# A roll along rows, DRAM to DRAM: 528 DMAs of one row per engine become sixteen DMAs of 32 rows per engine

## The chip, the cores and the metric

The kernel runs on one core of one Trainium2 chip. The metric is the device time of one execution in microseconds (us). The kernel before takes 826.24 us, the median of 3 runs (825.08 to 826.99).

A core has compute engines (TensorE, VectorE = DVE, ScalarE = ACT, GpSimd = POOL), SyncE (SP), and 16 DMA engines that copy memory. A DMA is started by an instruction on SP, ACT or POOL; its transfer is then cut into packets that the 16 DMA engines carry out. Here SP and ACT each have one hardware queue, and POOL has a software queue. Almost nothing is computed in this kernel: it is a copy of 268 MB from DRAM to DRAM with every row rotated.

## The reference

```python
def setup_inputs():
    return {
        "x": np.random.randn(8192, 8192).astype(np.float32),
        "shift": 100,
    }

def reference(x: np.ndarray, shift: int) -> np.ndarray:
    return np.roll(x, shift, axis=1)
```

Output column `c` of a row is input column `c - 100`, and the first 100 output columns are the last 100 input columns of the same row. A row has 8192 floats, 32 KB.

## The kernel before

With `shift` 100 the kernel sets `s = 100`, `a = 128` (the shift rounded up to a multiple of 128) and `g = a - s = 28`. Output columns 128 to 8191 are the *long pieces*: 8064 floats (32,256 bytes) of each row, copied from input columns 28 to 8091. Output columns 0 to 127 are the *heads*: 100 floats from the end of the input row and 28 from its start.

**Long pieces (lines 27 to 36).** The rows are taken in 256 blocks of 32. Of a block, the 16 even rows go into one DMA issued by SP and the 16 odd rows into one DMA issued by ACT. In the view `(c e j) w -> c j e w`, `c` is the block, `j` even or odd, and `e` one of 16 rows. As `e` is the slowest dimension of the transfer, each of the 16 DMA engines gets one row of it: one piece of 32,256 bytes. In the last 8 blocks each row is cut in two (columns 128 to 4095 and 4096 to 8191), and each half goes in a DMA of its own. So there are 248 DMAs of whole pieces and 16 of halves on each of the two queues, 528 in all. They run straight from `x` to `out` in DRAM and pass through no on-chip memory.

No line of the kernel waits between these DMAs. The framework gives DMAs on the hardware queues eight semaphores in turn, four for each issuing engine. A DMA may only be issued when the earlier one with the same semaphore has landed on all 16 DMA engines. So each queue has at most four of these DMAs in flight, and the fifth waits for the first.

**Heads (lines 50 to 68).** POOL handles them, 512 rows at a time, in 16 steps of four rows per partition. Line 60 loads a tile `t` of 128 x 3 x 128 floats: a run of 128 floats that begins 100 before a row's end holds the end of one row and the start of the next. Lines 61 and 64 load into the tile `h` what these runs don't hold. DVE copies from `t` to `h` (lines 62 and 65). After all 16 steps, line 68 writes the 16 tiles `h` to the first 128 columns of `out`. These DMAs are issued with `single_packet`, and at most eight are in flight.

Both parts write different columns of `out` and read only `x`, so neither waits for the other. They share the 16 DMA engines and the DRAM.

Of the kernel before, what the change touches and what calls it, by code (L numbers as in the profile page):

```python
# [1 line left out]

# [4 lines left out]


@with_exitstack
def kernel(  # L10
    ctx: ExitStack,
    tc: tile.TileContext,
    x: bass.AP,
    shift: int,
    out: bass.AP,
):
    nc = tc.nc
    n_rows, n_cols = x.shape
    s = shift % n_cols
    a = -(-s // 128) * 128  # L20
    g = a - s
    P = nc.NUM_PARTITIONS
    engines = [nc.sync, nc.scalar]
    n_chunks = 16
    rows = n_rows // n_chunks

    xm = x.rearrange("(c e j) w -> c j e w", e=16, j=2)
    om = out.rearrange("(c e j) w -> c j e w", e=16, j=2)
    if a < n_cols:
        blocks = n_rows // 32  # L30
        mid = (a + n_cols) // 256 * 128
        for c in range(blocks):
            parts = ((a, mid), (mid, n_cols)) if c >= blocks - 8 and a < mid else ((a, n_cols),)
            for j in range(2):
                for lo, hi in parts:
                    engines[j].dma_start(out=om[c, j, :, lo:hi], in_=xm[c, j, :, lo - s:hi - s])
    if a == 0:
        return

    if a > 512:  # L40
        for i in range(n_chunks):
            r = slice(i * rows, (i + 1) * rows)
            nc.gpsimd.dma_start(out=out[r, :s], in_=x[r, n_cols - s:])
            if g > 0:
                nc.gpsimd.dma_start(out=out[r, s:a], in_=x[r, :g])
        return

    Q = 4
    n_st = n_rows // (P * Q)
    reads = ctx.enter_context(tc.tile_pool(name="reads", bufs=n_st))  # L50
    heads = ctx.enter_context(tc.tile_pool(name="heads", bufs=n_st))
    xt = x.rearrange("(k p q) c -> k p q c", q=Q, p=P)
    ot = out.rearrange("(k p q) c -> k p q c", q=Q, p=P)
    tiles = []
    for k in range(n_st):
        t = reads.tile([P, Q - 1, a], x.dtype)
        h = heads.tile([P, Q, a], x.dtype)
        lead = bass.AP(tensor=x.tensor, offset=(k * P * Q + 1) * n_cols - s,
                       ap=[[Q * n_cols, P], [n_cols, Q - 1], [1, a]])
        nc.gpsimd.dma_start(out=t[:], in_=lead, single_packet=True)  # L60
        nc.gpsimd.dma_start(out=h[:, Q - 1, :s], in_=xt[k, :, Q - 1, n_cols - s:], single_packet=True)  # L61
        nc.vector.tensor_copy(h[:, :Q - 1, :s], t[:, :, :s])  # L62
        if g > 0:
            nc.gpsimd.dma_start(out=h[:, 0, s:], in_=xt[k, :, 0, :g], single_packet=True)  # L64
            nc.vector.tensor_copy(h[:, 1:, s:], t[:, :, s:])  # L65
        tiles.append(h)
    for k, h in enumerate(tiles):
        nc.gpsimd.dma_start(out=ot[k, :, :, :a], in_=h[:], single_packet=True)  # L68


# [1 line left out]
_INS = ['x', 'shift']  # L72
_OUTS = [((8192, 8192), 'float32')]

_NUMBERS = {'shift': 100}


# [26 lines left out]
```

## Time and profile before

| | |
|---|---|
| median of the runs | 826.24 us |
| the profiled execution, its own time | 825.38 us |
| its span (first to last instruction) | 823.6 us |
| DRAM read, written | 268.44 MB, 268.44 MB |
| packets on the two hardware queues | 8448 each: 4224 of data, 4224 of 4 bytes |
| packets on POOL's queue | 3328: 2304 of data, 1024 of 4 bytes |
| POOL busy | 41.1 us |
| DVE busy | 7.8 us |

The profile's page gives, for 40 slices of the span, how busy the DMA engines were (9 is 90% or more) and what they moved. It then lists the DMA queues: `q1` and `q10` are the two hardware queues (SP's and ACT's), `q0` is POOL's. A packet of 4 bytes is the write that tells a semaphore that one DMA engine has done its part of a DMA. The list of issues gives for each kind of DMA how many there were, their size, and the median time from issue to landing. GB/s counts each byte moved once; a copy from DRAM to DRAM loads the DRAM with twice that. Besides the page, the trace holds a record of every packet (queue, start, duration, size) and of every write to a semaphore; it does not say which DMA engine a packet ran on.

### The profile page before, as it was taken

Reading aid. Unit: us, or ns where it says so; the run is one execution under the profiler, and the core shown is the slowest. Engines: PE = TensorE matmul, PEld = TensorE weight load, DVE = VectorE, ACT = ScalarE, POOL = GpSimd, SP = SyncE. Lnnn points to the kernel's source line nnn. Section 1 sums busy time; section 2 is a strip of 40 time slices with the busy share of each in tenths; the row PEclk is TensorE's granted clock in tenths of the full one; section 3 lists DMA queues with packets and bytes.
Section 4 is the critical chain, followed back from the end, with each engine's and each line's share of the span. In section 5 each row is a group of like instructions: output and inputs, shape, how many; then the busy total and the mean of one; then the engine's idle time right before and its main releaser. Section 6 shows DMA issues by size and latency. Waiting matters only on the chain. (4 is left out here: it accounts for less than half of the span.)

```text
span 823.6 us, 689 instructions
## 1 busy us (share of the span) xinstructions
DVE 7.8 (1%) x32; POOL 41.1 (5%) x68
## 2 busy tenths in 40 slices
DVE  0000000000000000000000000000000000000000
POOL 3111111211100000000000000000000000000000
DMA  9999999999999999999999999999999999999998
GB/s 300 345 338 345 325 338 340 332 344 359 341 341 345 338 337 323 332 332 321 329 331 331 324 329 331 332 326 329 332 326 329 336 323 337 320 335 337 321 312 302
DMA packets 20229, 272.71 MB, mean 331 GB/s; under 512 B 9472, under 2 KB 9728, under 8 KB 11776
## 3 DMA queue, kind: packets, MB, share of 16 engines
q1 hardware_dynamic: 8448, 132.14, 47.8%
q10 hardware_dynamic: 8448, 132.14, 46.7%
q0 software_dynamic: 3328, 8.39, 4.7%
q14 instruction: 5, 0.04, 0.0%
HBM read 268.44 MB, written 268.44 MB: 652 GB/s over the span
## 5 line engine op out<-in xcount | busy, mean ns | idle before, releaser
L68 POOL DMA_DIRECT2D out_dram<-h x16 | 11.4, 712 | 83.1 <-DMA out_dram<-h 49.6
L60 POOL DMA_DIRECT2D t<-in_x_dram x16 | 12.1, 758 | 32.5 <-DMA h<-in_x_dram 31.6
L64 POOL DMA_DIRECT2D h<-in_x_dram x16 | 8.6, 539 | 80.4 <-DMA t<-in_x_dram 80.4
L61 POOL DMA_DIRECT2D h<-in_x_dram x16 | 8.9, 558 | 20.8 <-DMA h<-in_x_dram 20.8
L62 DVE COPY h<-t 128x300 f32<-128x300 f32 x16 | 5.9, 368 | 179.7 <-DMA t<-in_x_dram 179.7
L65 DVE COPY h<-t 128x84 f32<-128x84 f32 x16 | 3.2, 201 | 0.0
L85 POOL MEMSET const-float32-0.0<- 128x1 f32 x1 | 0.1, 99 | 0.2 <-issue 0.2
L85 POOL MEMSET const-bfloat16-1.0<- 128x1 bf16 x1 | 0.1, 101 | 0.0
L85 POOL MEMSET const-uint8-127<- 128x1 uint8 x1 | 0.1, 99 | 0.0
L85 POOL MEMSET const-float32-1.0<- 128x1 f32 x1 | 0.1, 98 | 0.0
## 6 DMA issues: line engine op xcount, KB each, us to landing
out_dram<-in_x_dram ACTq DMA_DIRECT2D x248, 504.0 KB, 12.6
out_dram<-in_x_dram SPq DMA_DIRECT2D x248, 504.0 KB, 12.6
out_dram<-h POOLq DMA_DIRECT2D x16, 256.0 KB, 64.9
t<-in_x_dram POOLq DMA_DIRECT2D x16, 192.0 KB, 31.6
out_dram<-in_x_dram ACTq DMA_DIRECT2D x8, 256.0 KB, 6.0
out_dram<-in_x_dram SPq DMA_DIRECT2D x8, 256.0 KB, 5.9
out_dram<-in_x_dram ACTq DMA_DIRECT2D x8, 248.0 KB, 6.1
out_dram<-in_x_dram SPq DMA_DIRECT2D x8, 248.0 KB, 6.1
```

The lines of the kernel that those rows point to most:

```text
L60: nc.gpsimd.dma_start(out=t[:], in_=lead, single_packet=True)
L61: nc.gpsimd.dma_start(out=h[:, Q - 1, :s], in_=xt[k, :, Q - 1, n_cols - s:], single_packet=True)
L62: nc.vector.tensor_copy(h[:, :Q - 1, :s], t[:, :, :s])
L64: nc.gpsimd.dma_start(out=h[:, 0, s:], in_=xt[k, :, 0, :g], single_packet=True)
L65: nc.vector.tensor_copy(h[:, 1:, s:], t[:, :, s:])
L68: nc.gpsimd.dma_start(out=ot[k, :, :, :a], in_=h[:], single_packet=True)
L85: nc = _bacc.Bacc("TRN2", target_bir_lowering=False, num_devices=1)
```

## The change

The long pieces are issued as sixteen DMAs, eight by SP and eight by ACT. The rows are taken in 8 blocks of 1024. Of each block a DMA takes all even or all odd rows, `16 x 32` of them: each DMA engine gets 32 pieces, one of each of the 32 former blocks, in the same order. The halves in the last 8 former blocks are gone. The rest of the kernel is unchanged; its line numbers are three lower.

```diff
-    xm = x.rearrange("(c e j) w -> c j e w", e=16, j=2)
-    om = out.rearrange("(c e j) w -> c j e w", e=16, j=2)
     if a < n_cols:
-        blocks = n_rows // 32
-        mid = (a + n_cols) // 256 * 128
-        for c in range(blocks):
-            parts = ((a, mid), (mid, n_cols)) if c >= blocks - 8 and a < mid else ((a, n_cols),)
+        deep = 32
+        xm = x.rearrange("(b c e j) w -> b j e c w", c=deep, e=16, j=2)
+        om = out.rearrange("(b c e j) w -> b j e c w", c=deep, e=16, j=2)
+        for b in range(n_rows // (32 * deep)):
             for j in range(2):
-                for lo, hi in parts:
-                    engines[j].dma_start(out=om[c, j, :, lo:hi], in_=xm[c, j, :, lo - s:hi - s])
+                engines[j].dma_start(out=om[b, j, :, :, a:], in_=xm[b, j, :, :, a - s:n_cols - s])
```

The semaphores are dealt out as before: on each queue the first four DMAs are issued at once, and the fifth waits until the first has landed on all 16 engines.

## The prediction

> **What bounds the kernel now.** I read the page's slices first, then the DMA queues, the waits of SP's queue, stretches of the span by time, and last the trace's records of packets and semaphore writes.
>
> ```profile
> DMA  9999999999999999999999999999999999999998
> GB/s 300 345 338 345 325 338 340 332 344 359 341 341 345 338 337 323 332 332 321 329 331 331 324 329 331 332 326 329 332 326 329 336 323 337 320 335 337 321 312 302
> ...
> q1 hardware_dynamic: 8448, 132.14, 47.8%
> q10 hardware_dynamic: 8448, 132.14, 46.7%
> q0 software_dynamic: 3328, 8.39, 4.7%
> ...
> HBM read 268.44 MB, written 268.44 MB: 652 GB/s over the span
> ```
>
> The DMA engines are busy from end to end (47.8 + 46.7 + 4.7 = 99.2%), at a rate that hardly moves. Nothing else in the program is near a limit. But is it the engines or the DRAM? The packet records decide: an unhindered piece of 32,256 bytes takes 1193 ns (the shortest, and 5% of all), 27.0 GB/s on one engine, 432 GB/s on 16; between 320 and 770 us the mean is 1556 ns, the 95th percentile 2080. So a piece is usually held up by something shared. The stretches say by what:
>
> ```profile
> core 0: us, DVE busy (x) POOL busy (x), PEclk, DMA share, GB/s
> ...
> 20.00:190.00 170.00, 7.28 (x30) 28.11 (x45) 1.00 1.00 339
> 190.00:320.00 130.00, 0.00 (x0) 6.40 (x9) 1.00 1.01 341
> 320.00:794.00 474.00, 0.00 (x0) 0.00 (x0) 1.00 1.00 329
> 794.00:819.50 25.50, 0.00 (x0) 0.00 (x0) 1.00 0.92 313
> 819.50:823.60 4.10, 0.00 (x0) 0.00 (x0) 1.00 0.52 178
> ```
>
> The last two columns are the engines' busy share and GB/s. With POOL's traffic (first two rows) more bytes move, but POOL's bytes touch DRAM once and a long piece's twice; counted by DRAM traffic from the packet records, the rates are about 648, 657 and 658 GB/s. One number fits three mixes: the DRAM side caps the kernel near 658 GB/s, 329 GB/s of copying, and 329/27.0 = 12.2 unhindered engines would be enough to reach it.
>
> ```profile
> SPq L36 <- DMA out_dram<-in_x_dram: 678.2, 260, 4.6
> ...
> out_dram<-in_x_dram ACTq DMA_DIRECT2D x248, 504.0 KB, 12.6
> out_dram<-in_x_dram SPq DMA_DIRECT2D x248, 504.0 KB, 12.6
> ```
>
> SP waited 260 times (264 DMAs less the first four) for an earlier DMA to land: the window of four. It couples the engines. For the 300 DMAs that landed between 320 and 790 us the median spread between the first and the last of the 16 engines is 5.5 us: thirteen within 2.5 us, the last two 3 to 5.5 us behind. The leaders run into the window: from 20 to 790 us about 0.5% of the 16 engines' time has no packet open. Under a cap that costs nothing, as the others take the bandwidth. In the last 25 us the halves shrink the spread to 1.6 us.
>
> **The change, part by part.**
>
> *The floor, unchanged.* 264.2 MB of long pieces at 329 GB/s are 803.2 us; POOL's 8.39 MB at 658 GB/s are 12.8 us. Together 816.0. The span has 7.6 more: the start, 5 x (1 - 206/329) = 1.9 (206 GB/s in the first 5 us), the end, 25.5 x (1 - 313/329) + 4.1 x (1 - 178/329) = 1.2 + 1.9 = 3.1, and 2.6 under POOL's traffic.
>
> *Issues and waits removed:* 256 issues on each of SP and ACT, and 252 waits on each. Nothing else is queued on SP or ACT, and the rings were rarely dry, so 0. From below: the 0.5% idle, 4.1 us, if it was real loss.
>
> *Semaphore writes removed.* Each engine carries two 4-byte packets (about 6 ns each by the starts that follow one another) per pair of pieces; 256 pairs x 12 ns = 3.1 us per engine. Under the cap this is again bandwidth that others use: 0 taken, -3.1 at best.
>
> The Trainium skill's "DMA: Bandwidth & Descriptors" (Rules for kernel authors, with its fit of 2.0 us fixed per DMA) says to move a MiB or more per DMA; 512 DMAs fewer would by that fit be 1024 us of fixed cost, an estimate of 128 us with eight in flight. The trace disagrees: that cost lies under other packets, since the engines idle 0.5%.
>
> *POOL's turns.* A 4-byte packet took a turn on its engine like a piece did: the packet records, followed along one engine, read: a piece of q1, a piece of q10, POOL, 4 bytes of q1, 4 bytes of q10, POOL. So POOL had two turns per pair. It used 3328/16 = 208 turns per engine between 5.3 and 321.1 us, 1.52 us each. With one 4-byte packet in 32 it gets one turn per pair, so 208 of the 256 pairs: its heads last until 640 to 690 us rather than 321. That is still inside the bulk, 130 us early; the cover is the long pieces, and if it went, see the last rival. Cost 0.
>
> *The start.* Which order the descriptors of a deep DMA appear in is not shown. q10's first 16 packets start in two groups 0.66 us apart, at 41 ns per packet if that is generation. From below 0; from above, if the 32 of one engine come before the next engine's, the last engine starts 480 x 0.041 = 20 us late, about +14 at both ends together. The page shows 16 pieces starting inside 0.8 us, the nearest row, so I take 0.
>
> *The end: the window opens.* Four DMAs of 32 pieces on two queues are 256 pieces, 400 us of work: no engine waits for another any more, and each simply has 512 pieces and its POOL packets to do. Pieces vary with a standard deviation of 298 ns (packet records, 330 to 770 us), POOL's 144 data packets per engine with 324 ns. If they vary independently, engines end with a deviation of sqrt(512) x 0.298 = 6.7 and sqrt(144) x 0.324 = 3.9, together 7.8 us. The last of 16 is then some 1.8 deviations, 14 us, behind the mean. Once four engines have finished, the others run unhindered, 1193 instead of 1556 ns; over the last 25 us this wins back 25 x 0.23 = 6. Loss at the end: 14 - 6 = 8 us, in place of 3.1. Bounds: the spread of now, 5.5 us in two engines, loses about 3.2; the largest, a lag that belongs to certain engines, is a rival below.
>
> *Sum* on the profiled execution: 825.4 - 3.1 + 8.0 = 830.3 us, +0.6%. That run lies 0.9 us under the median of 826.24, against which it is +0.5%.
>
> **Rivals.**
>
> *Nothing drifts.* Were the equal mean pace due to the DRAM alone, the spread would stay at 5.5 us: 825.4 - 3.1 + 3.2 = 825.5. For it: the chains of packets that can be followed for 200 us and more have mean pieces of 1550 to 1574 ns, under 2% apart. Against: rings that run dry, so a window that does hold the leaders.
>
> *Faster.* If the engines' own occupancy is the limit and not the DRAM, every gap removed counts: 0.5% idle (4.1), semaphore writes (3.1), the halves' stretch and its end (some 2.5 of 3.1): 825.4 - 9.7 = about 816. It decides if pieces keep their mean of 1556 ns when the gaps are gone. For it: a busy share of 1.00 everywhere. Against: 1193 ns possible, and one DRAM rate in three mixes.
>
> *Slow engines run away.* Between the 12th and 24th DMA (27 to 49 us) the spread grew from 2.2 to 7.0 us, then the window stopped it. About 15 turns of POOL fell in it, 0.33 us per turn; if it is the same few engines each time, the 128 turns of POOL's loads give 128 x 0.33 = 42 us. Three engines 42 us late work alone at the end: some 27 pieces too many each at 1193 ns, 32 us, less what the others did not have to do in the shared stretch, about 8: +24. 825.4 - 3.1 + 24 = 846. For it: the last three of 16 stand apart in every stretch. Against: long POOL packets (275 of 2304 over 500 ns) are found in nearly every chain. The skill's same page (Latency and other measured facts) calls engines 7 and 15 usually slower under descriptors from GpSimd, a best guess there. No record here names an engine, so the trace neither confirms nor denies it.
>
> *POOL starves.* If a queue's turn lasted for all 32 pieces of a DMA, POOL would get 8 turns and do its 200 others behind the bulk: 16 steps of loads and writes with 41.1 us of POOL's own time and landings, some 60 us, less the 12.8 us of DRAM traffic moved there: 825 + 47 = 872. Against: each piece has a packet of its own now.
>
> **How the numbers follow.** Forecast 0.45; nothing drifts 0.17; faster 0.18; run-away 0.13; starved 0.07. Three runs spread by 0.2%, so a change below 0.2%, 824.6 to 827.9, counts as none. Faster: 0.18 + 0.02 of the undrifted = 0.20. Same: 0.14 of the undrifted + 0.06 of the forecast's low end = 0.20. Slower: 0.60. The range reaches from the faster case to the run-away one, 816 to 846, and leaves out the starved case and the far sides; the forecast's own is 826 to 838.
>
> **What would show it.** Right: the same 329 GB/s in mid-run, hardly any 4-byte packets, POOL's last packet at 640 to 690 us, the engines' last landings spread over 15 us or more, and GB/s falling in the last slices. Wrong: a rate above 332 or below 326 GB/s in mid-run (the DRAM cap depends on the order that the window kept), a last landing as tight as now, POOL's packets after the bulk, or a slow first 20 us.

## The result: slower by 3.4%, and the profile after

The changed kernel takes 862.34 us (median of 6 runs, 851.69 to 880.34) against 825.49 us for the kernel before in the same rounds (824.67 to 826.99). The ratio is 1.0338, 95% interval 1.0314 to 1.0363; as its times scatter by 3%, this ratio (and each below that has an interval) is made from the runs within 1.5% of the kernel's fastest, here three of six (851.69 to 856.67), and the ratio of the medians of all runs is 1.045. The profiled execution took 877.91 us, with a span of 876.1: what follows shows the effect at its larger size.

The page of the changed kernel, its slices, packets and queues:

```profile
DMA  9999999999999999999999999999999999998310
GB/s 304 341 324 335 331 334 330 331 336 331 329 336 329 332 331 337 328 334 323 330 330 333 340 334 341 337 335 339 331 338 335 329 319 327 324 327 315 137 46 25
DMA packets 11777, 272.64 MB, mean 311 GB/s; under 512 B 1280, under 2 KB 1536, under 8 KB 3584
...
q10 hardware_dynamic: 4224, 132.12, 44.1%
q1 hardware_dynamic: 4224, 132.12, 43.7%
q0 software_dynamic: 3328, 8.39, 5.2%
```

36 slices run at some 330 GB/s, near the rate before. The last three collapse to 137, 46 and 25 GB/s. The 4-byte packets of the hardware queues are all but gone (1280 packets under 512 bytes, most of them POOL's, where there were 9472), the bytes are the same, and POOL's packets take 5.2% of the engines' time where they took 4.7%. The stretches of the changed kernel (busy share and GB/s in the last columns):

```profile
core 0: us, DVE busy (x) POOL busy (x), PEclk, DMA share, GB/s
640.00:780.00 140.00, 0.00 (x0) 0.00 (x0) 1.00 1.00 328
780.00:800.00 20.00, 0.00 (x0) 0.00 (x0) 1.00 0.98 326
800.00:820.00 20.00, 0.00 (x0) 0.00 (x0) 1.00 0.60 239
820.00:840.00 20.00, 0.00 (x0) 0.00 (x0) 1.00 0.20 87
840.00:860.00 20.00, 0.00 (x0) 0.00 (x0) 1.00 0.09 37
860.00:876.00 16.00, 0.00 (x0) 0.00 (x0) 1.00 0.06 24
```

A busy share of 0.06 is one engine of 16. Against 329 GB/s the rows lose 0.2 + 5.5 + 14.7 + 17.8 + 14.8 = 53 us. The span grew by 52.5, and the end of the kernel before had lost 3.1, so the end accounts for 50 of the 52.5: in the last DMA twelve engines are done between 797 and 822 us, three more by 848, and one works alone until 875.

When they fell apart shows in the writes to semaphores, 16 for each DMA, one by each engine. For the changed kernel's profiled execution, in us of the span (six of the sixteen DMAs; the median engine is the middle of the 16 landings):

| DMA (its last landing) | first to last engine | the last four, behind the median engine |
|---|---|---|
| 115 | 16.6 | 2.0, 4.7, 10.3, 10.7 |
| 237 | 43.0 | 10.7, 22.0, 26.1, 34.8 |
| 361 | 73.0 | 26.5, 27.0, 27.5, 57.9 |
| 488 | 103.0 | 23.7, 24.4, 45.5, 81.7 |
| 592 | 104.4 | 26.6, 27.8, 47.9, 84.1 |
| 796 | 102.3 | 26.4, 26.5, 46.8, 82.0 |

In the kernel before the spread was 5.5 us in mid-run. Here it grows evenly to 488 us and then stops. POOL's last load packet starts at 477 us; its writes go on until 730 us and add nothing. In the packet records many load packets are long: 258 of the 768 of 4096 bytes (34%), and 41% of those of 3200 bytes, take over 500 ns, while the quickest take 159 and 125 ns. They are not spread evenly. The trace doesn't name a packet's engine, but a packet starts within nanoseconds of the end of the one before it on its engine, so chains of packets can be followed, with some wrong links. Between 120 and 240 us the three slowest chains, with load packets of 0.9 to 1.3 us on average, do 0.52 to 0.60 pieces per us; nearly all others, with load packets of 0.25 to 0.6 us, do 0.62 to 0.68. After the loads all packets of POOL take about 159 ns and all chains do 0.62 to 0.63.

### The profile page after: what moved, and what is told of

It reads as the page before. It is cut to its first block, busy times and chain, and to the rows that moved or that the text cites. A ratio compares the mean times of both kernels' runs of the same rounds, so it can differ in the third digit from the quotient of the medians.

```text
span 876.1 us, 177 instructions
## 1 busy us (share of the span) xinstructions
DVE 7.8 (1%) x32; POOL 41.1 (5%) x68
## 2 busy tenths in 40 slices
DMA packets 11777, 272.64 MB, mean 311 GB/s; under 512 B 1280, under 2 KB 1536, under 8 KB 3584
## 4 chain that ended last, share of the span: by engine, by line
another core or an unknown queue 61%; DMA 5%; POOL 1%; issue 1%; DVE 1%; POOLq 0%; DVEq 0%; PEldq 0%
DMA t<-in_x_dram 5%; POOL out_dram L65 1%; DVE h L59 1%; DVE h L62 0%; POOL t L57 0%; POOLq L96 0%; POOL h L58 0%; POOL h L61 0%; POOLq L65 0%; DVEq L96 0%; PEldq L96 0%
```

## Experiments

Theory L, formed from this: POOL's loads are slow on a few DMA engines, these engines fall behind for as long as loads run, and the deep DMAs take away the window that held the others back. The runs were made on several chips (the kernel before takes 815 to 827 us on them), so each is given as a ratio to the kernel before on the same chip.

**1 and 2. Both kernels without the heads.** POOL's and DVE's work is left out.

```diff
-    if a == 0:
-        return
+    return
```

> The changed kernel without the heads: POOL loads, DVE copies and POOL writes are left out, the first 128 output columns stay unwritten. Theory L (POOL's load packets are slow on a few DMA engines and, with no window of four short DMAs, these engines fall behind all through the loads): without loads nothing falls behind; 803 us of copying at 329 GB/s, 1.9 at the start, an end of 3 to 8, 1.8 around the span: 810 to 816 us, last landings within 15 us of each other. Rival D (deep DMAs let the engines drift whatever else runs): landings spread over 50 us and more, 830 us and more.

> The kernel before without the heads, the control of the run above. Theory L and rival D both: 803 + 1.9 + 3.1 + 1.8 = about 810 us; L has it within 5 us of the changed kernel without heads, D has it 20 us or more faster.

Measured: changed kernel 803.05 us, ratio 0.9829 (0.9804 to 0.9853); kernel before 804.26 us, ratio 0.9846 (0.9829 to 0.9864). The page of the changed kernel without heads:

```profile
DMA  9999999999999999999999999999999999999997
GB/s 311 333 332 327 337 327 338 333 328 337 332 338 328 332 332 343 327 332 332 337 327 333 337 335 327 333 333 335 330 327 328 337 335 327 335 330 332 330 337 250
```

No tail: one slice ends at 250 GB/s. Its engines land within 4.6 us of each other in the first DMA and 8.7 us in the last; over 800 us, with a window of 128 pieces per engine and queue, 16 engines drift apart by no more than 12, and the last is never more than 3.2 us behind the median. Deep DMAs cost nothing by themselves, and save nothing that can be told from zero. Rival D falls. Both times lie under the bands (the chip was a faster one: 816.47 us for the kernel before), the difference between the two is as expected.

**3. Four pieces per engine and DMA.**

```diff
-        deep = 32
+        deep = 4
```

> The changed kernel with 4 pieces per engine and DMA instead of 32 (128 DMAs, no halves). The window is then 4 x 4 pieces on each of two queues, 32 x 1.5 = 48 us of work, less the time that a new DMA needs. Theory L: the lag grows until the window stops it, at 35 to 45 us in the last landings, and the end costs 15 to 25 us in place of 3: 835 to 848 us, with less scatter between runs than the changed kernel. Rival H (what is lost is the short pieces at the end): as the changed kernel, 850 us or more.

Measured: 836.83 us, ratio 1.0236 (1.0183 to 1.0290). The spread grows to 37.5 us at 218 us, reaches 44 us at most and stays at 36 to 42 from 324 us to 810, though loads go on until 357 us: the window stops it where it should. The slices end with `285 68`. The ratio lies in the band (835 to 848 us on a chip of 825).

**4. No halves.** One part of the change alone, on the kernel before: DMAs of one piece per engine to the end.

```diff
-            parts = ((a, mid), (mid, n_cols)) if c >= blocks - 8 and a < mid else ((a, n_cols),)
+            parts = ((a, mid), (mid, n_cols)) if False else ((a, n_cols),)
```

> The kernel before with whole pieces to the end (512 DMAs of one piece per engine, no halves): one part of the change alone. Theory L: the window holds the spread at 5 to 7 us, and the end costs 1 to 3 us more than with halves: 824 to 829 us. Rival H (the halves are what the changed kernel misses): 840 us or more.

Measured: 818.77 us, ratio 1.0022 (1.0006 to 1.0038); the last DMA spreads by 5.2 us rather than 1.1. The halves are worth 0.2%, and rival H falls.

**5 and 6. Short DMAs first, or last.** Run 5 issues 64 blocks as DMAs of one piece and the rest as deep ones; run 6 five deep DMAs on each queue and the last 96 blocks as DMAs of one piece, with halves (`od` and `xd` are the views for deep DMAs). Run 5, against the changed kernel:

```diff
+        ahead = 2
...
-        for b in range(n_rows // (32 * deep)):
...
+        for c in range(ahead * deep):
             for j in range(2):
-                engines[j].dma_start(out=om[b, j, :, :, a:], in_=xm[b, j, :, :, a - s:n_cols - s])
+                engines[j].dma_start(out=om[c, j, :, a:], in_=xm[c, j, :, a - s:n_cols - s])
+        for b in range(ahead, n_rows // (32 * deep)):
+            for j in range(2):
+                engines[j].dma_start(out=od[b, j, :, :, a:], in_=xd[b, j, :, :, a - s:n_cols - s])
```

Run 6, against the kernel before:

```diff
+        deep = 32
+        ahead = 5
...
+        for b in range(ahead):
+            for j in range(2):
+                engines[j].dma_start(out=od[b, j, :, :, a:], in_=xd[b, j, :, :, a - s:n_cols - s])
...
-        for c in range(blocks):
+        for c in range(ahead * deep, blocks):
```

> The first 64 of the 256 former blocks (some 200 us, in which POOL's loads run) as DMAs of one piece per engine, the other 192 blocks as deep DMAs of 32 pieces, no halves. Theory L (load packets of POOL that are slow on a few engines make these fall behind where no window holds the others): the spread stays under 10 us in the first part and grows little after it; 0.998 to 1.008 of the kernel before. Rival H (deep DMAs to the end cost the time, by their last landings): as the changed kernel, 1.03 or more.

> The other way round: five deep DMAs on each queue (160 former blocks, through all of the loads), then DMAs of one piece per engine for the last 96 blocks, with halves in the last 8 as before. Theory L: the engines are some 50 to 100 us apart when the short DMAs begin, and at that point the leaders run dry until the last engine has come: the loss is made in mid-run and nothing gives it back; 1.02 to 1.045 of the kernel before, with a dip in GB/s near 500 to 600 us. Rival H (short pieces at the end are what counts): 1.00 to 1.005.

Measured: run 5 821.4 us, ratio 1.0074 (1.0052 to 1.0096); run 6 851.02 us, ratio 1.0339 (1.0284 to 1.0395), the same as the whole change. In run 5 the spread stays at 4 to 9.5 us under the loads and is 18 at the end, but through two engines that run ahead: the last is 2 us behind the median. Run 6 ends like the kernel before, with its last landings 1.3 us apart, and has lost the time elsewhere. Its stretches:

```profile
core 0: us, DVE busy (x) POOL busy (x), PEclk, DMA share, GB/s
200.00:480.00 280.00, 4.36 (x18) 18.60 (x29) 1.00 1.00 337
480.00:500.00 20.00, 0.00 (x0) 1.42 (x2) 1.00 0.99 340
500.00:520.00 20.00, 0.00 (x0) 0.72 (x1) 1.00 0.60 240
520.00:540.00 20.00, 0.00 (x0) 1.42 (x2) 1.00 0.28 114
540.00:560.00 20.00, 0.00 (x0) 0.71 (x1) 1.00 0.16 64
560.00:840.00 280.00, 0.00 (x0) 1.42 (x2) 1.00 0.99 332
```

The hole of the changed kernel's end has moved to 500 to 560 us, where the short DMAs make the leaders wait for the last engine. Against 329 GB/s its three stretches lose 35 us, of the 42 by which this execution (856.58 us) lies above the kernel before. The loss is the lag that grew under the loads, and it is paid at whatever point the engines must meet.

**7. Writes only.** POOL's loads are left out; DVE fills `h` with zeros.

```diff
-        nc.gpsimd.dma_start(out=t[:], in_=lead, single_packet=True)
...
+        nc.vector.memset(h[:], 0.0)
```

> The changed kernel without POOL's loads: DVE fills the tiles h with zeros instead, and POOL writes them (the first 128 output columns are zeros). Theory L: writes have no slow packets (159 ns each in the changed kernel's trace), last landings within 15 us, the time of the kernel before less 6 us of DRAM traffic: 0.990 to 0.998. Rival W (any POOL traffic spreads the engines, loads and writes alike): landings 40 us and more apart, 1.01 or more.

Measured: 807.34 us, ratio 0.9907 (0.9884 to 0.9929). No packet of POOL takes over 500 ns (mean 160). First to last landing reaches 21 us at the end, over the band of 15, but through engines that run ahead, by up to 19 us: the last is 2.4 us behind the median. Rival W falls. Loads make the lag, writes do not.

**8. Loads from one contiguous stretch.** The heads then hold other values of `x`.

```diff
-        lead = bass.AP(tensor=x.tensor, offset=(k * P * Q + 1) * n_cols - s,
-                       ap=[[Q * n_cols, P], [n_cols, Q - 1], [1, a]])
+        lead = bass.AP(tensor=x.tensor, offset=k * P * Q * a,
+                       ap=[[Q * a, P], [a, Q - 1], [1, a]])
...
```

> The changed kernel with POOL's loads reading one contiguous stretch of x (4 MB) instead of places 32 KB apart, same sizes of descriptors, same destinations; the first 128 output columns then hold other values. Theory A (it is the addresses: reads a row apart meet in the same part of the DRAM): the packets over 500 ns become rare, the spread stays under 30 us, 1.00 to 1.01 of the kernel before. Theory P (it is the path: loads into on-chip memory by the software queue are slow on certain engines, from wherever they read): a quarter or more of the load packets still over 500 ns, the spread 60 us and more, 1.02 to 1.05.

Measured: 817.07 us, ratio 1.0029 (1.0014 to 1.0045). The tail is gone:

```profile
GB/s 315 340 330 336 344 341 340 340 333 329 342 342 337 340 331 341 343 340 338 341 338 345 338 345 341 335 346 342 345 335 344 332 328 338 333 335 333 331 327 249
```

Of the 3200-byte packets 0.8% take over 500 ns rather than 41%, of all load packets 6% rather than 29%, and the spread is 7.8 us at 513 us, 12 at the end. All of the 3.4% but what the missing halves cost (0.2%, run 4) is gone with the addresses of 4 MB of loads changed. One thing was not as the expectation says: three rows of 512 bytes that lie behind one another become one piece of 1536 bytes, so for `t` the pieces changed too (its largest packets, now of 4608 bytes, are still over 500 ns in 12% of cases); for the other loads only the addresses did.

**9. Loads shifted by 256 bytes per partition.** Other values in the heads again.

```diff
-                       ap=[[Q * n_cols, P], [n_cols, Q - 1], [1, a]])
+                       ap=[[Q * n_cols + 64, P], [n_cols, Q - 1], [1, a]])
...
```

> The changed kernel with each partition's loads moved on by 64 floats (256 bytes) against the partition before; still four rows (128 KB) and a little more apart, same sizes, same alignment within 256 bytes, same destinations; the first 128 output columns then hold other values. Theory A (all loads of the heads meet at one place modulo the row length of 32 KB, and reads there are slow for a few engines): packets over 500 ns become rare, spread under 30 us, 1.00 to 1.01 of the kernel before. Rival F (what made the contiguous loads fast was that they were close together, not that they differed modulo 32 KB): as the changed kernel, over a quarter above 500 ns, 1.02 to 1.05.

Measured: 868.06 us (867.01 to 868.82), ratio 1.0618 (1.0594 to 1.0642). Neither theory A's time nor rival F's fits. The page:

```profile
GB/s 278 289 301 294 310 287 296 309 300 286 292 300 294 308 289 306 303 298 292 288 336 339 345 335 343 342 347 339 342 337 348 333 337 330 330 334 328 337 330 273
...
q0 software_dynamic: 3328, 8.39, 13.8%
```

No tail, and 21 us at most from first to last landing. The loss is in the first half, at 298 GB/s where it had been 330. Now 756 of the 768 4096-byte load packets are over 500 ns (mean 1.6 us), so on every engine: loads hold an engine for 108 us in sum on average, against 35 in the changed kernel, and pieces are quicker (1350 ns on average from 20 to 420 us, 1469 in the changed kernel). With the engines busy all the time (a share of 1.00) and the pieces quicker, this reads as a limit by the engines' time and no longer by the DRAM; no run tested that by itself. Slow loads shared evenly cost 6%, by another way than lag. One kind of load went the other way, as theory A has it: of the 3200-byte packets 3% are over 500 ns, where it was 41%. So the same shift made some loads quick and others slow, and neither theory covers that.

**10. Half of the loads.** Steps 8 to 15 load nothing; DVE fills their tiles with zeros.

```diff
+        if k < n_st // 2:
...
+        else:
+            nc.vector.memset(h[:], 0.0)
```

> The changed kernel with loads for the first 8 of the 16 steps only; DVE fills the other eight tiles with zeros, and all 16 are written (zeros in half of the rows' first 128 columns). Theory L, with the lag made packet by packet: half the lag, some 40 to 55 us between first and last landing, and half the loss: 1.010 to 1.020 of the kernel before, after 3 us less of DRAM traffic. Rival T (the lag comes at the start and is then only kept): as the changed kernel, 80 us and more, 1.03.

Measured: 839.79 us, ratio 1.0237 (1.0171 to 1.0303). The spread is 49.8 us at 244 us, when the loads are over, half of 104. The last engine is then 40 us behind the median and 27 from mid-run on. The spread grows again, to 61 us at 744 us, but at the other end: one engine runs from 10 to 34 us ahead of the median, mostly after POOL's last packet; why is not shown. So the lag is made packet by packet; the loss lies above the band of 1.010 to 1.020, its interval reaches into it.

**11. Two pieces per engine and DMA.**

```diff
-        deep = 32
+        deep = 2
```

> Two pieces per engine and DMA (256 DMAs, no halves): the window is 4 x 2 pieces on each of two queues, some 25 us of work. Theory L: the spread is stopped at 15 to 20 us, 1.006 to 1.014 of the kernel before, between the kernel without halves (1.002) and four pieces (1.024).

Measured: 825.27 us, ratio 1.0093 (1.0056 to 1.0131); spread mostly 17 to 20 us from 150 us on. With the runs above this gives a ladder of windows: one piece 1.0022, two 1.0093, four 1.0236, thirty-two 1.0338.

**12. The kernel before with the contiguous loads** of run 8 (same diff, on the kernel before).

> The kernel before with the contiguous loads of the eighth run (first 128 output columns hold other values). Theory L: the window already takes up what slow loads do, so nothing is won: 0.996 to 1.002. Rival C (slow loads cost the kernel before as well): 0.985 to 0.995.

Measured: 817.33 us, ratio 1.0000 (0.9983 to 1.0016). The kernel before has 28% of its 4096-byte load packets over 500 ns and pays nothing for them that can be measured.

**13. Rows turned round among the engines.** From step to step the loads read rows 0, 128, 256 or 384 further on or back; the heads hold other rows' values.

```diff
+        turn = (k % 4) * 128 * (1 if k < 12 else -1)
...
-        lead = bass.AP(tensor=x.tensor, offset=(k * P * Q + 1) * n_cols - s,
+        lead = bass.AP(tensor=x.tensor, offset=(k * P * Q + turn + 1) * n_cols - s,
...
```

> The changed kernel with the rows that POOL loads moved by 0, 128, 256 or 384 rows (0, 4, 8 or 12 MB, the rows of 0, 4, 8 or 12 engines) from one step to the next; pitch, columns, sizes and destinations as in the changed kernel; the heads of most rows then hold those of other rows. Theory E (certain DMA engines are slow at such loads, whatever the row): spread of 80 us and more after the loads, 1.03 or more. Theory R (certain rows are slow, and with the fixed pattern the same engine gets them at every step): the slow loads fall on all engines in turn, spread under 40 us, 1.00 to 1.015, with as many packets over 500 ns as before.

Measured: 862.33 us (846.76 to 874.0) against 826.56, a ratio of the medians of 1.043. The spread is 43 us at 241 us, as in the changed kernel, but 68 at 564 us, where that had 104. Theory R in its plain form (under 40 us, 1.015) does not hold, theory E asked for 80 us: with one profile of each, and times that overlap, it stays open whether the engine alone decides.

## Why the prediction was wrong

The floor, the issues and the semaphore writes came out as written: 328 GB/s in mid-run after the loads, deep DMAs that neither save nor cost (runs 1 and 2). That 3.1 us of semaphore writes per engine and 0.5% of idle are worth nothing under the cap also holds, as far as 803.05 against 804.26 us can show it. The rival *faster* fell with that. The fit of 2.0 us per DMA, which the prediction sets against the trace, stands in the Trainium skill's "DMA: Bandwidth & Descriptors" (Anatomy of one DMA) for DMAs issued by GpSimd; the merged ones here were issued by SP and ACT, so 1024 us was no estimate for them.

POOL's one turn per pair was right in kind: its loads last 477 us rather than 190, its last packet ends at 730 us, 40 us later than the 640 to 690 forecast. Whether it costs 0 was not tested alone. The number of load packets, with which the lag grew in run 10, is the same as before; but more of them are long (41% of the 3200-byte packets rather than 18.8%), and the runs don't show why. The start cost nothing, as taken: the first 5 us moved 206 GB/s, as before.

The step that failed is *The end: the window opens*, at the words "If they vary independently, engines end with a deviation of ... 7.8 us". It took the last engine to be 14 us behind and the loss at the end to be 8 us. Measured: 84 us behind the median engine at most (75 behind the mean), and a loss of 53 us at the end of the profiled run (the medians differ by 37). Both halves of that sum were wrong, in opposite directions. The pieces, which gave 6.7 of the 7.8 us, hardly make an engine late: without heads the last is at most 3.2 us behind the median in 800 us (run 1), and *nothing drifts* is the right account of the late end. Engines do run ahead (by 19 us in run 7, 34 in run 10; why is not shown), but run 7 was no slower than its band for it. POOL's loads, which stand behind the 3.9, are not chance that evens out: some engines get more of the long packets for as long as the loads run, and a lag that adds up goes with the number of packets (half the loads, half the spread, run 10) and not with its root.

The mechanism stood among the rivals as *slow engines run away*, with a chance of 0.13, 42 us of lag and 846 us. Its row, the growth from 2.2 to 7.0 us before the window caught it, was the one to believe; the true lag was twice as large. The argument against it, that long load packets are found in nearly every chain, is true of the changed kernel too: what counts is not whether an engine gets long packets but how many more than the others. What that trace did show, and the prediction passed over, is a share: 18.8% of the 3200-byte packets were over 500 ns and the others mostly near 126. *POOL starves* did not occur.

The cause is shown on three sides: take away the loads (runs 1, 7), change their addresses (run 8) or keep the window while they run (runs 4, 5), and the loss goes; put the short DMAs after them (run 6), and it stays. Two things stay open: why loads at these addresses are long, and whether it is the engine, the row or both that decides who gets them (run 13). No version that moves all the bytes beats the kernel before: without its halves, with other loads, or with deep DMAs after the loads only, it comes out at 1.000 to 1.007 of it.

## What to carry to other kernels

Many short DMAs in a small window do two jobs, and only one of them is visible as waits: they also keep 16 engines in step, so that an engine that is slow at something else is waited for at once, and what the leaders leave of the bandwidth goes to it. Here that cost nothing that could be measured (run 12). Before merging them, look at the spread of an engine's landings per DMA while each kind of side traffic runs; a spread that grows until the window stops it is the lag that will add up without the window. Estimate such a lag by its growth per packet times the number of packets that cause it, not as chance.

## What was not expected of the hardware

- Small strided loads can hold an engine ten times as long as they need: 512-byte pieces 32 KB apart, and 128 KB from partition to partition, took 159 ns per 4096-byte packet at best and over 500 ns in 34% of the packets. With 256 bytes more from partition to partition (run 9) the 4096-byte packets took 1.6 us on average, while the packets of 3200 bytes fell from 553 ns to 158. Close together (run 8) the 3200-byte packets took 137. Which property of the addresses does this was not settled.
- A 4-byte semaphore write takes a turn on its engine like a piece of 32 KB. Followed along the chains, POOL gets one packet per pair of pieces in the changed kernel (0.99), where it got two or a little more, and its writes land later. Before and after:

```profile
out_dram<-h POOLq DMA_DIRECT2D x16, 256.0 KB, 64.9
...
out_dram<-h POOLq DMA_DIRECT2D x16, 256.0 KB, 122.4
```

- Sixteen engines that only copy from DRAM to DRAM at the shared limit kept in step by themselves within 12 us over 800 (run 1). With other traffic before or beside it, one or two engines ran ahead, by 19 us in run 7 and 34 in run 10, while the last stayed 2.4 us behind the median in run 7.
